# Moving the float32r tiles of an encoder layer to multiples of 512 bytes

## Chip, core and metric

The kernel runs on one core of one Trainium2 chip. The metric is the device time of one execution in microseconds (us). Before the change three runs took 2624.37, 2624.96 and 2625.81 us; the median, 2624.96, is the time to compare with.

## What is computed

One encoder layer on 256 tokens of 2048 channels, in float32. `lnorm` is a layer norm, ALPHA is 2 ** 0.25.

```python
h = lnorm(ALPHA * h + 0.5 * swiglu(h, ffn1_w_in, ffn1_w_out))   # d_ff = 5632
proj = h @ mix_w_in                                             # 2048 x 18944
y_a = hgrn2_both_directions(proj[...]) @ w_a                    # 16 heads of 128
y_b = dilated_attention(proj[...]) @ w_b                        # 3 groups of 4 heads
h = lnorm(ALPHA * h + (g_a * y_a + g_b * y_b) @ mix_w_out)
h = lnorm(ALPHA * h + 0.5 * swiglu(h, ffn2_w_in, ffn2_w_out))
```

All large products are of a [256, K] activation with a weight matrix that is read once from memory, 474 MB in all.

## The kernel before

**Precision.** Every operand of a large product is split into a high and a low part, both of type float32r (`H` is the value rounded to float32r, `L` is what is left), and the product is the sum of three: high by high, high by low, low by high. Activations are kept transposed, channels on partitions: `xH`/`xL` (input of a stage), `hH`/`hL` (hidden layer of a swiglu), `zH`/`zL` (gated sum of the mixer), `oBH`/`oBL` (attention output).

**Order of the work.** `Job` (line 43) is one block of output columns. `run` (line 181) walks through the jobs and cuts the weights of each into chunks of 2048 values per partition, 1 MB. `load` (line 148) fetches a chunk with one DMA into `raw` (three buffers), and splits it, half by half, into `wH` (ScalarE) and `wL` (VectorE, line 165), four buffers of each. `run` loads the chunks of one step ahead. A chunk of a block of 1024 columns feeds 24 matmuls of 512 columns at line 217: two rows of 128 channels, three products, two token tiles of 128, two halves of the block. The activation is the stationary operand (128x128) and the weights are the moving one (128x512):

```python
nc.tensor.matmul(out=job.ps[t, j], lhsT=job.lhs(a, k, t),
                 rhs=b[:, o + j * 512:o + (j + 1) * 512], start=first, stop=last)
```

In the jobs marked `dims` (line 229) it is the other way round: weights stationary, 256 columns of `xH` or `xL` moving. In the attention's projection `lhs` is `parity` (line 762): every second token, so the stationary operand is read with a step of two elements. Each matmul instruction comes with its own load of the stationary operand, also where two in a row use the same one.

The last chunks of three jobs (`room` in `load`, lines 400 and 925) don't have their split weights in `wH`/`wL` but in tiles called `early`, which lie in other pools.

The recurrence and the attention itself work on float32 tiles (lines 653 to 687, 808, 816), and `transpose4` (line 101) transposes with the identity matrix `ident` as the moving operand.

**Where the tiles lie.** Pools are stacked in the order in which they are opened, and a pool's tiles in the order in which their names first appear. The tile `ident` is at byte 16512 of each partition. Behind it come the other constants, `vecs` (512 bytes) among them, then the pools `wraw` (`raw`), `wsp` (`wH`, `wL`), `big` (`acc`, `xH`, `xL`), `small` (statistics and scratch, 1248 bytes), and from byte 127520 on the pools of the stages. So the starting addresses, as remainders of a division by 512 and by 64, are:

| tiles | pool | mod 512 | mod 64 |
|---|---|---|---|
| `raw`, `wH`, `wL`, `acc`, `xH`, `xL` | wraw, wsp, big | 320 | 0 |
| `hH`, `hL`, `silu`, `early`, `zH`, `zL`, `oBH`, `oBL`, `z` | pools of the stages | 32 | 32 |
| `ident` | const | 128 | 0 |
| float32 tiles of the recurrence | hgrn | 288, 320 or 352 | 32, 0 or 32 |

Within a tile all operands of line 217 start at multiples of 512 bytes (128 tokens of 4 bytes, or 512 columns), but for `parity`, whose second token tile starts 4 bytes later than the first.

The change touches the constants and pools at lines 86 to 92 and the line `vecs = const.tile(...)` at 426. `vecs` holds five short vectors that are loaded, transposed once (`lower_bounds`) and not used again, all in the first microseconds of the kernel.

Of the kernel before, what the change touches and what calls it, by code (L numbers as in the profile page):

```python
# [10 lines left out]
F32 = mybir.dt.float32  # L11
# [6 lines left out]
P = 128  # L18
# [24 lines left out]
class Job:  # L43
    """One block of output columns: out[tok, C] = sum over nk tiles of x^T W.

    head/tail: this many of the first/last chunks run one token tile after the other.
    room: gives room for a chunk's split weights outside the pool for them, or None.
    mid: called after the first step; hook: before the last token tile meets the last chunk.
    dims: the block comes out transposed, out[col, tok], two heads to a bank.
    """  # L50

# [18 lines left out]
def kernel(ctx, tc, x, ffn1_in, ffn1_out, ln1_g, ln1_b, mix_in, lb_fwd, lb_bwd,  # L70
# [3 lines left out]
    x, out = x[0], out[0]  # L74
# [3 lines left out]
    const = ctx.enter_context(tc.tile_pool(name="const", bufs=1))  # L78
# [3 lines left out]
    small = ctx.enter_context(tc.tile_pool(name="small", bufs=2))  # L82
# [9 lines left out]
    acc = big.tile([P, NT, D], F32, name="acc")  # L92

    def new_x():
        return (big.tile([P, KD, SEQ], F32R, tag="xH", name="xH"),
                big.tile([P, KD, SEQ], F32R, tag="xL", name="xL"))
# [4 lines left out]
    def transpose4(srcs):  # L101
        ps = tp_tile()
        for i, s in enumerate(srcs):
            nc.tensor.transpose(out=ps[:, i * P:(i + 1) * P], in_=s, identity=ident)  # L104
        return ps

    def split(ps, H, L):
        """H + L = ps exactly, both in float32r."""
        nc.scalar.copy(out=H, in_=ps)  # L109
        nc.vector.tensor_sub(out=L, in0=ps, in1=H.bitcast(F32))  # L110

    def rsqrt(y, v, n):
        """y = v ** -0.5 for [P, n] (v is positive): a guess from the exponent and three Newton steps."""
        z = small.tile([P, n], F32, tag=f"rs{n}", name="rsz")
        nc.vector.tensor_scalar(y.bitcast(I32), v.bitcast(I32), 1, None, op0=OP.logical_shift_right)
        nc.vector.tensor_scalar(y.bitcast(I32), y.bitcast(I32), -1.0, MAGIC, op0=OP.mult, op1=OP.add)
        for i in range(3):
            if n == 1:
                nc.vector.scalar_tensor_tensor(z, y, v, y, op0=OP.mult, op1=OP.mult)
            else:  # L120
                nc.vector.tensor_mul(z, y, y)
                nc.vector.tensor_mul(z, z, v)
            # the factor -2 of each of the first two steps stays in y, and is taken out in the last
            if i < 2:
                nc.vector.scalar_tensor_tensor(y, z, -3.0 * 4.0 ** i, y, op0=OP.add, op1=OP.mult)
            else:
                nc.vector.tensor_scalar(z, z, -768.0, -1.0 / 8192.0, op0=OP.add, op1=OP.mult)
                return nc.vector.tensor_mul(y, y, z)
# [17 lines left out]

# [1 line left out]
    def load(job, r, parts=1):  # L148
# [25 lines left out]
    def fence(ins):  # L174
        """What is traced from here to the end of this step or, if that is sooner, of the next
        goes to the vector engine behind ins."""
        es = ExitStack()
        es.enter_context(tc.issue_after(ins.ins))
        fences.append([es, 2])
# [95 lines left out]
    def to_x(src, xo, t, c):  # L275
        """Columns c * 512... of token tile t, in src [P, 512], to the transposed H and L."""
        ps = transpose4([src[:, i * P:(i + 1) * P] for i in range(4)])
        ts = slice(t * P, (t + 1) * P)
        split(ps.rearrange("p (k s) -> p k s", k=4), xo[0][:, 4 * c:4 * c + 4, ts], xo[1][:, 4 * c:4 * c + 4, ts])

# [1 line left out]
    stats = {}  # L282
# [6 lines left out]
    class LayerNorm:  # L289
# [32 lines left out]
        def tile(self, t):  # L322
            """Token tile t of acc is complete."""
            if t == 1:
                for c, u in self.got.items():
                    self.apply(0, c, u)
            self.begin(t)
            if t == 0:
                if not self.lead:
                    self.apply(0, 0)  # L330
            elif self.dst is not None:
                self.rest([(1, c) for c in range(4)])
            elif self.lead:
                self.rest([(1, 0), (1, 1), (0, 2), (1, 2), (0, 3), (1, 3)])
            else:
                self.rest([(1, 0)] + [(tt, c) for c in range(1, 4) for tt in range(NT)])

        def first(self):
            """The last tile is nearly complete."""
            for c in range(2 if self.dst is None else 4):  # L340
                self.got[c] = self.scale(0, c)
# [10 lines left out]

# [1 line left out]
    def ffn(w_in, w_out, cur, pool, before, tpost, post, hook):  # L354
# [66 lines left out]

# [1 line left out]
    cur["x"] = new_x()  # L423
    pl = {}
    pl["ffn"] = open_pool("ffn1")
    vecs = const.tile([P, P], F32, name="vecs")

# [53 lines left out]

# [1 line left out]
    ln = {}  # L483
# [19 lines left out]

# [1 line left out]
    hs = {}  # L505
# [42 lines left out]
    def hgrn_pair(g, pr, st):  # L548
# [15 lines left out]
        def flat(ap, t, b, f):  # L564
            """[P, h * t, u] or, for one t, [P, h, u] of half f of block b."""
            if t is None:
                return ap.rearrange("p (g b f u) -> p g b f u", b=2, f=2, u=HCHUNK)[:, :, b, f, :]
            return v6(ap)[:, :, t, b, f, :]
# [4 lines left out]
        q = st["q", pr]  # L573
        f = {0: st["f", pr], 1: st["b", pr]}
        d1s, d1e = hs["d1s"], hs["d1e"]
        K1, Q1, KC, QC = t512("k1"), t512("q1"), t512("kc"), t512("qc")
        # direction d: inc is the decay from the chunk's entry up to and with a token, exc the decay
        # from behind a token to the chunk's end; entry and end are those of the direction's time
        KS, QR, inc, K2, Q2 = {}, {}, {}, {}, {}
        for d in range(2):  # L580
            k = t512("k")
# [3 lines left out]
            a = inc[d] = t512(f"i{d}")  # L585
# [17 lines left out]
            yield 1.7  # L603
            # near half: the one that the direction enters first
            nr, fr = (0, 1) if d == 0 else (1, 0)
# [6 lines left out]
        for d in range(2):  # L612
            # keys of block bk meet queries of block bq of the same tile, keys of tile bk queries of tile bq
            nr, fr = (0, 1) if d == 0 else (1, 0)
            bk, bq = nr, fr
            T = inc[d].rearrange("p (c u) -> p c u", u=HCHUNK)[:, :, 31:32] if d == 0 else c32(inc[d])[:, :, 0:1]
# [26 lines left out]

        # scores, keys on partitions
        def tok(ap, h, t):
# [28 lines left out]
        ATo = p.tile([P, 2, 2, P], F32, tag="ato", name="ato")  # L674
# [3 lines left out]
        for h in range(2):  # L678
            hl = 2 * pr + h
            hd = 4 * g + hl  # L680
            v = st["v"]
            for t in range(NT):
                o = po[:, (2 * h + t) * P:(2 * h + t + 1) * P]
                nc.tensor.matmul(out=o, lhsT=ATd[h][:, t, :], rhs=v[:, t, hl * P:(hl + 1) * P],  # L684
                                 start=True, stop=False)
                # ATo[:, h, 0]: keys of tile 0, queries of tile 1; [:, h, 1] the other way
                nc.tensor.matmul(out=o, lhsT=ATo[:, h, 1 - t, :], rhs=v[:, 1 - t, hl * P:(hl + 1) * P],  # L687
                                 start=False, stop=True)
# [70 lines left out]

    # attention: columns of group g are q, k, v of 512; tile 0 has the even tokens and tile 1 the odd ones,  # L760
    # so that the second and third group attend only within a tile
    def parity(x, k, t):
# [75 lines left out]

    # branch gates
    def gate_evac(key, blk):  # L840
# [95 lines left out]
    for blk in range(2):  # L936
        jobs.append(Job(mix_out, 0, KD, blk * 1024, 1024, lambda: (hs["zH"], hs["zL"]), mo_evac(blk),
                        tpost=ln2_tile if blk == 1 else None, post=ln2 if blk == 1 else None, tail=4 * blk,
                        room=ln2_room if blk == 1 else None, hook=lambda: ln[2].first()))

# [1 line left out]
    def ln3_before():  # L942
        ln[3] = LayerNorm(load_gb(pl["ffn"], ln3_g[0], ln3_b[0]), pl["ffn"], None, out, lead=True)

    ffn2 = ffn(ffn2_in, ffn2_out, cur, lambda: pl["ffn"], ln3_before, lambda t: ln[3].tile(t), close_pool,
               lambda: ln[3].first())
# [53 lines left out]
```

## Time and profile before

| | |
|---|---|
| median of three runs | 2624.96 us |
| span of the profiled execution, first to last instruction | 2623.6 us |
| TensorE matmul busy | 2600.1 us, 99%, 12889 instructions |
| TensorE load of the stationary operand busy | 2187.8 us, 83%, 12889 instructions |
| VectorE busy | 1533.4 us, 58% |
| ScalarE busy | 1155.7 us, 44% |
| DMA | 483 MB, 184 GB/s, 54% of the engines' time |
| mean granted TensorE clock | 0.999 |

The page gives no other time for the profiled execution than its span, so what lies around the span is taken as its distance to the median, 1.4 us. The records of two successive matmuls overlap (a matmul of 512 columns has a record of about 390 ns, and the next one begins before it ends). The time that a matmul costs is therefore not its duration but the distance from its start to the next one's start: the length of a stretch in which TensorE never idles, divided by the number of matmuls that start in it.

### The profile page before, as it was taken

The page shows a single profiled execution, that of the slowest core. Times are in us where ns is not written, and L with a number is a line of the kernel's source. Part 1 is how long each engine was busy: PE and PEld are TensorE (multiplying, and loading weights), DVE is VectorE, ACT ScalarE, POOL GpSimd, SP SyncE. Part 2 cuts the span into 40 slices and gives each one's busy share as a digit, 9 for nine tenths or more (in the row PEclk, how much of TensorE's full clock was granted, in tenths as well). Part 3 has the DMA queues.
Part 4 walks back from the last instruction along what each step waited for, and adds up shares of the span by engine and source line. Part 5 has one row for each costly group of instructions (what it writes and reads, how often), then busy time and mean ns, then how long its engine had stood idle before and what let it go on. Part 6 is the DMA issues. An engine that isn't in the chain of part 4 may idle for free.

```text
span 2623.6 us, 31518 instructions
## 1 busy us (share of the span) xinstructions
PE 2600.1 (99%) x12889; PEld 2187.8 (83%) x12889; DVE 1533.4 (58%) x1865; ACT 1155.7 (44%) x1395; POOL 4.8 (0%) x28
## 2 busy tenths in 40 slices
PE   8999999999999999999999999999999999999998
PEld 7888888888889999998888888888788888888886
DVE  5455555454585877878544544556755455555557
ACT  5444343444444455554544544444444444444442
POOL 0000000000000000000000000000000000000000
PEclk9999999999999999999999999999999999999999
DMA  7555555555655544544555445656555555555563
GB/s 243 187 184 192 192 192 179 193 190 192 211 174 177 177 162 145 174 163 161 188 177 183 154 162 193 191 191 213 172 193 191 193 178 192 191 192 181 193 220 129
DMA packets 147281, 483.32 MB, mean 184 GB/s; under 512 B 7664, under 2 KB 7872, under 8 KB 146368
## 3 DMA queue, kind: packets, MB, share of 16 engines
q1 hardware_dynamic: 145680, 473.99, 54.4%
q10 hardware_dynamic: 1456, 7.32, 0.7%
q8 instruction: 101, 1.65, 0.2%
q14 instruction: 44, 0.36, 0.0%
HBM read 479.17 MB, written 2.10 MB: 183 GB/s over the span
## 4 chain that ended last, share of the span: by engine, by line
PE 97%; DVE 2%; DMA 0%; ACT 0%; issue 0%; SPq 0%; DVEq 0%; ACTq 0%
PE ps L217 82%; PE ps L229 10%; PE tp L104 2%; PE tp L653 1%; PE tp L657 1%; DVE wL L165 0%; DVE lnu L307 0%; PE tp L687 0%; DVE lnu L311 0%; DMA acc<-in_x 0%; PE tp L808 0%; PE tp L816 0%; DVE st L287 0%; PE tp L684 0%; PE tp L672 0%; ACT wH L165 0%
## 5 line engine op out<-in xcount | busy, mean ns | idle before, releaser
L165 DVE TENSOR_TENSOR wL<-raw,wH 128x1024 fp32r<-128x1024 f32 x884 | 1078.1, 1222 | 1007.8 <-ACT wH L165 1006.3
L165 ACT CAST wH<-raw 128x1024 fp32r<-128x1024 f32 x884 | 929.0, 1052 | 1291.5 <-PE ps L217 1157.0
L217 PE MATMUL ps<-wH,xH 128*128 128x512 f32 x2336 | 748.1, 391 | 1.7 <-ACT xH L109 1.7
L217 PE MATMUL ps<-wL,xH 128*128 128x512 f32 x2336 | 749.0, 391 | 0.0
L217 PE MATMUL ps<-wH,xL 128*128 128x512 f32 x2336 | 748.6, 391 | 0.3
L217 PEld LDWEIGHTS ps<-wH,xH 128*128 128x128 f32 x2336 | 440.0, 189 | 92.5 <-ACT xH L109 2.8
L217 PEld LDWEIGHTS ps<-wH,xL 128*128 128x128 f32 x2336 | 440.2, 189 | 92.1 <-DVE xL L110 1.8
L217 PEld LDWEIGHTS ps<-wL,xH 128*128 128x128 f32 x2336 | 439.6, 189 | 89.9
L217 PE MATMUL ps<-wL,hH 128*128 128x512 f32 x672 | 216.7, 399 | 0.0
L217 PE MATMUL ps<-wH,hH 128*128 128x512 f32 x672 | 212.0, 396 | 0.0
L217 PE MATMUL ps<-wH,hL 128*128 128x512 f32 x672 | 210.9, 395 | 0.0
L217 PEld LDWEIGHTS ps<-wH,hL 128*128 128x128 f32 x672 | 126.0, 188 | 29.8
L217 PEld LDWEIGHTS ps<-wH,hH 128*128 128x128 f32 x672 | 125.2, 188 | 29.7
L217 PEld LDWEIGHTS ps<-wL,hH 128*128 128x128 f32 x672 | 125.3, 188 | 29.0
L229 PE MATMUL ps<-xH,wH 128*128 128x256 f32 x768 | 125.8, 285 | 0.0
L229 PE MATMUL ps<-xL,wH 128*128 128x256 f32 x768 | 124.8, 284 | 0.0
L229 PE MATMUL ps<-xH,wL 128*128 128x256 f32 x768 | 124.8, 284 | 0.0
L229 PEld LDWEIGHTS ps<-xH,wH 128*128 128x128 f32 x768 | 106.5, 192 | 0.3
L229 PEld LDWEIGHTS ps<-xH,wL 128*128 128x128 f32 x768 | 106.3, 192 | 0.0
L229 PEld LDWEIGHTS ps<-xL,wH 128*128 128x128 f32 x768 | 106.3, 192 | 0.0
L385 DVE SCALAR_TENSOR_TENSOR acc<-ps,acc 128x512 f32<-128x512 f32 x96 | 60.3, 680 | 1.3 <-PE ps L217 1.3
L217 PE MATMUL ps<-wL,zH 128*128 128x512 f32 x112 | 35.4, 397 | 0.0
(181 smaller groups left out, 1244.7 us busy)
## 6 DMA issues: line engine op xcount, KB each, us to landing
raw<-in_ffn_w_in SPq DMA_DIRECT2D x175, 1024.0 KB, 5.0
raw<-in_mix_w_in SPq DMA_DIRECT2D x148, 1024.0 KB, 5.1
raw<-in_ffn_w_out SPq DMA_DIRECT2D x88, 1024.0 KB, 5.3
raw<-in_w_branch_a SPq DMA_DIRECT2D x16, 1024.0 KB, 5.3
raw<-in_mix_w_out SPq DMA_DIRECT2D x16, 1024.0 KB, 5.4
raw<-in_w_branch_b SPq DMA_DIRECT2D x4, 1024.0 KB, 5.3
gbt<-in_ln_g ACTq DMA_DIRECT2D x3, 1024.0 KB, 7.2
gbt<-in_ln_b ACTq DMA_DIRECT2D x3, 1024.0 KB, 10.0
```

What stands on the lines that cost most here:

```text
L104: nc.tensor.transpose(out=ps[:, i * P:(i + 1) * P], in_=s, identity=ident)
L165: both = nc.scalar.copy(out=H, in_=s), nc.vector.tensor_sub(out=L, in0=s, in1=H.bitcast(F32))
L217: nc.tensor.matmul(out=job.ps[t, j], lhsT=job.lhs(a, k, t), rhs=b[:, o + j * 512:o + (j + 1) * 512], start=first, stop=last)
L229: nc.tensor.matmul(out=job.ps[h // 2][:, (h % 2) * SEQ:(h % 2 + 1) * SEQ], lhsT=b[:, o + h * P:o + (h + 1) * P], rhs=a[:, k, :], start=fir ...
L385: nc.vector.scalar_tensor_tensor(a, ps, 0.5, a, op0=OP.mult, op1=OP.add)
L653: nc.tensor.matmul(out=pa[:, (d * NT + t) * P:(d * NT + t + 1) * P], lhsT=tok(KS[d], h, t), rhs=tok(QR[d], h, t), start=True, stop=True)
L657: nc.tensor.matmul(out=pc[:, (i * NT + t) * P:(i * NT + t + 1) * P], lhsT=tok(a, h, t), rhs=tok(b, h, t), start=True, stop=True)
```

## The change

Two tiles are added that nothing writes or reads: `fill` of 48 float32 values (192 bytes) among the constants, and `fill` of 72 values (288 bytes) at the front of `small`. `vecs` moves from the constants to the front of the pool `ffn1`. Everything behind the constants thus moves down by 320 bytes and everything behind `small` by 32. Addresses after: `raw`, `wH`, `wL`, `acc`, `xH`, `xL` and all of `hH`, `hL`, `silu`, `early`, `zH`, `zL`, `oBH`, `oBL`, `z` start at a multiple of 512. `ident` stays at 128. The float32 tiles of the recurrence go from 288, 320, 352 to 256, 288, 320. The strided second token tile of `parity` starts at 4. No instruction is added, removed or given another operand; the rest of the diff takes out comments.

```diff
     acc = big.tile([P, NT, D], F32, name="acc")
 
+    const.tile([P, 48], F32, name="fill")
+    small.tile([P, 72], F32, name="fill", bufs=1)
+
     def new_x():
...
     pl["ffn"] = open_pool("ffn1")
-    vecs = const.tile([P, P], F32, name="vecs")
+    vecs = pl["ffn"].tile([P, P], F32, name="vecs")
```

## Rows read from the trace of the kernel before

**Rows 1.** The page's busy times by engine.
```profile
span 2623.6 us, 31518 instructions
...
PE 2600.1 (99%) x12889; PEld 2187.8 (83%) x12889; DVE 1533.4 (58%) x1865; ACT 1155.7 (44%) x1395; POOL 4.8 (0%) x28
```

**Rows 2.** The page's chain of work that ended last, shares of the span by engine.
```profile
PE 97%; DVE 2%; DMA 0%; ACT 0%; issue 0%; SPq 0%; DVEq 0%; ACTq 0%
```

**Rows 3.** Who waited for whom on TensorE: us in total, times, longest.
```profile
PE tp L104 <- DMA acc<-in_x: 8.6, 2, 4.3
PE ps L217 <- ACT xH L109: 1.7, 4, 0.4
PE tp L104 <- ACT ast L774: 0.2, 1, 0.2
```

**Rows 4.** Busy time of each engine in three stretches in which TensorE does nothing but matmuls of line 217: the first with `xH`/`xL` as stationary operand, the second with `hH`/`hL`, the third with `oBH`/`oBL`; `wH`/`wL` moves in all. After the length come busy us and, in brackets, the instructions of PE, PEld, DVE, ACT and POOL, then the granted clock, the DMA engines' busy share and GB/s. The edges lie just ahead of a load, so the number behind PEld is that of the loads and thus of the matmuls that start in the stretch.
```profile
304.80:391.85 87.05, 87.05 (x385) 72.07 (x384) 43.71 (x41) 35.81 (x36) 0.00 (x0) 1.00 0.58 191
2392.10:2433.16 41.06, 41.06 (x177) 32.99 (x176) 21.50 (x21) 15.25 (x15) 0.00 (x0) 1.00 0.59 190
1668.14:1690.30 22.16, 22.16 (x96) 17.81 (x95) 16.91 (x17) 12.47 (x14) 0.00 (x0) 1.00 0.60 190
```

**Rows 5.** Timeline of TensorE's matmuls around the first chunk of `early` (moving) with `hH`/`hL` (stationary): start, us, instruction, count. The chunk begins at 733.65 and ends at 739.12.
```profile
733.65 1.09 PE L217 MATMUL ps<-early,hH 128*128 128x512 f32 x4
734.58 0.62 PE L217 MATMUL ps<-early,hL 128*128 128x512 f32 x2
735.04 1.07 PE L217 MATMUL ps<-early,hH 128*128 128x512 f32 x4
735.94 0.61 PE L217 MATMUL ps<-early,hL 128*128 128x512 f32 x2
736.40 0.62 PE L217 MATMUL ps<-early,hH 128*128 128x512 f32 x2
736.85 0.39 PE L217 MATMUL ps<-early,hL 128*128 128x512 f32 x1
737.08 0.62 PE L217 MATMUL ps<-early,hH 128*128 128x512 f32 x2
737.53 0.39 PE L217 MATMUL ps<-early,hL 128*128 128x512 f32 x1
737.76 0.62 PE L217 MATMUL ps<-early,hH 128*128 128x512 f32 x2
738.21 0.39 PE L217 MATMUL ps<-early,hL 128*128 128x512 f32 x1
738.44 0.62 PE L217 MATMUL ps<-early,hH 128*128 128x512 f32 x2
738.89 0.39 PE L217 MATMUL ps<-early,hL 128*128 128x512 f32 x1
739.12 0.63 PE L217 MATMUL ps<-wH,hH 128*128 128x512 f32 x2
```

**Rows 6.** Pieces of the chain that ended last, in order of time: start, us, what, matmuls. The first is a stretch of the recurrence's projection (256 columns moving), the second one of the attention's, with `parity` as stationary operand.
```profile
778.52 69.11 PE ps L229 x576
1359.56 43.87 PE ps L217 x188
```

**Rows 7.** Groups of instructions, matmuls by operands: count behind the x, then busy us and the mean ns of one record.
```profile
L217 PE MATMUL ps<-wL,xH 128*128 128x512 f32 x2336 | 749.0, 391 | 0.0
L217 PE MATMUL ps<-wL,hH 128*128 128x512 f32 x672 | 216.7, 399 | 0.0
L217 PE MATMUL ps<-wL,zH 128*128 128x512 f32 x112 | 35.4, 397 | 0.0
L217 PE MATMUL ps<-wL,oBH 128*128 128x512 f32 x32 | 10.1, 395 | 0.0
L229 PE MATMUL ps<-xL,wH 128*128 128x256 f32 x768 | 124.8, 284 | 0.0
```

**Rows 8.** The same view, the splitting of weights and activations on VectorE and ScalarE, into tiles at either place: count, busy us, mean ns, idle time before and who ended it.
```profile
L165 DVE TENSOR_TENSOR wL<-raw,wH 128x1024 fp32r<-128x1024 f32 x884 | 1078.1, 1222 | 1007.8 <-ACT wH L165 1006.3 <-DMA vecs<-in_hgrn_norm_g 0.6
L165 ACT CAST wH<-raw 128x1024 fp32r<-128x1024 f32 x884 | 929.0, 1052 | 1291.5 <-PE ps L217 1157.0 <-PE ps L229 108.3 <-issue 17.5
L165 DVE TENSOR_TENSOR early<-raw,early 128x1024 fp32r<-128x1024 f32 x12 | 14.1, 1218 | 3.3 <-ACT early L165 3.3
L165 ACT CAST early<-raw 128x1024 fp32r<-128x1024 f32 x12 | 12.0, 1049 | 6.2 <-DMA raw<-in_ffn_w_out 4.2 <-DMA raw<-in_mix_w_out 2.0
```

**Rows 9.** DMA issues: count, KB of one, median us from issue to landing.
```profile
raw<-in_ffn_w_out SPq DMA_DIRECT2D x88, 1024.0 KB, 5.3
```

## The prediction

> **What bounds the kernel now.** I read the busy times first: TensorE's matmuls cover 99% of the span [rows 1], and the chain that ended last is TensorE for 97% [rows 2]. TensorE hardly waits for anybody: 10.5 us in all, nearly all of it for the first input [rows 3]. So only two things can move the time much: fewer matmuls, of which the change has none, or less time from one matmul's start to the next. The question is whether that distance depends on where the operands lie, and the trace of before can answer it, because it already holds tiles at two kinds of places: 320 past a multiple of 512 bytes (a multiple of 64) and 32 past one.
>
> The second view is the stretches in which TensorE never idles [rows 4]. With `xH`, both operands at 320, 384 matmuls take 87.05 us: 226.7 ns each. With `hH`, stationary at 32 and moving still at 320, 176 take 41.06 us: 233.3 ns. With `oBH`, the same pair of places, 95 take 22.16 us: 233.3 ns. [...] So a matmul whose stationary operand lies at 32 costs 6.6 ns more.
>
> The third view tells which property does it. In the chunk with `early` as the moving operand [rows 5] both operands lie at 32, and from 735.04 to 739.12 us 18 matmuls take 4.08 us: 226.7 ns, as with both at 320. The same `hH` is dear with weights at 320 and cheap with weights at 32. So the price is not that of a tile at an odd place, but of two operands at **different** places; the load of one matmul's stationary operand runs while another's moving operand is being read, and the two seem to get in each other's way unless they are in step.
>
> [...]
>
> **The change, part by part.**
>
> *The places.* Afterwards all float32r tiles start at multiples of 512. Both operands of line 217 are then in step wherever the stationary one isn't strided, and I take the price of pairs in step, 226.7 ns, which two different places show [rows 4, 5].
>
> *How many gain.* Matmuls with a stationary `hH`/`hL`, `zH`/`zL` or `oBH`/`oBL` and `wH`/`wL` moving: three products each of 672, 112 and 32 [rows 7] make 2448. Some 40 of them follow a transpose or a chunk of `early`, and I leave them out: 2410. Gain 2410 x 6.6 = **15.9 us**, all of it on the path, since TensorE is the path. From below, counting the whole `early` chunk with its uneven start, 733.65 to 739.12, 24 matmuls take 5.47 us, 227.9 ns; the gain would be 2410 x 5.4 = 13.0 us.
>
> *Those already in step.* 2336 x 3 less the strided ones with `xH`, and 768 x 3 of 256 columns [rows 7], go from 320/320 to 0/0. No row shows a start at a multiple of 512. Two places that agree in nothing but being in step give one price, so I take no change; the bounds are the two rivals below.
>
> *The strided loads.* The attention's projection has 9 x 512 columns by 16 rows of channels by three products by two token tiles, 864 matmuls. They take 43.87 / 188 = 233.4 ns [rows 6], although their loads start at 320 or 324 with the moving operand at 320: a step of two goes out of step anyway. I take no change. Bounds: all come down to 226.7, 864 x 6.7 = 5.8 us gained, or as much lost.
>
> *Other engines.* Splitting a half chunk takes 1222 and 1052 ns into tiles at 320, 1218 and 1049 ns into `early` at 32 [rows 8]; VectorE and ScalarE don't care. I cost their moved tiles at nothing; both wait for TensorE for a large part of the span (ScalarE 1157 us [rows 8]), which is the cover.
>
> *The weight stream.* A faster TensorE asks for chunks sooner in the `hH` stretches: 24 x 226.7 = 5.44 us for a chunk instead of 5.60. A chunk of that matrix lands 5.3 us after its issue [rows 9] with three buffers in flight, and the `xH` stretch already runs at 5.44 us per chunk with a DMA share of 0.58 [rows 4]. So the gain isn't taken back by a late chunk. If this cover were gone, every chunk would take what it takes now and the gain would be zero.
>
> *The float32 tiles and the transposes.* The recurrence's tiles change places, `ident` does not. Together with the moved `vecs`, whose loads and transpose keep their instructions and queues, I cost them at nothing; a microsecond either way is possible and lies inside the bounds above.
>
> **Sum.** Profiled span 2623.6 - 15.9 = 2607.7 us; with the 1.4 us by which the median stands above that span, **2609.1 us**. Bounds: 13.0 - 5.8 = 7.2 us gained at least, 15.9 + 5.8 = 21.7 at most, so 2603.3 to 2617.8. What a measurement of this kernel can tell from no change is about 0.2%, 5.2 us.
>
> **The rivals.**
>
> *A. The multiple of 512 itself counts, and helps.* From 256 to 512 columns a matmul goes from 69.11 / 576 = 120.0 ns [rows 6] to 226.7, 106.7 for 256 columns. So 512 columns alone are 213.3 ns, and every float32r matmul carries 13.3 ns more, whatever its length. Both places of the trace make a 512-byte load run over a multiple of 512; after the change none does, and these 13.3 ns could be such a crossing. There are 9,600 matmuls of 512 and 2,304 of 256 columns: all of it gone would be another 11,904 x 13.3 = 158 us, 2451 us; half of it, 2530 us. For it: nothing in the trace excludes it. Against it: 320 and 32 cross at different points of the load and cost the same to a tenth of a nanosecond. I give it 0.10.
>
> [...]
>
> *B. Nothing happens.* Either the unused tiles get no room, so that everything stays at 320 and 32, or the price in the `hH` stretches comes from what else runs there and `early` is cheap by accident. Against it: three stretches at 233.3 to 233.4, two at 226.7, and VectorE busy in the cheap and the dear ones. Time 2625.0. I give it 0.08. [...]
>
> *C. Starting at a multiple of 512 makes moving reads and loads collide.* Place: the same matmuls that are now in step, 11,904 - 2,410 - 864 = 8,630. It decides from 15.9 us / 8,630 = 1.8 ns per matmul on; at one more step of 6.6 ns it costs 57 us, and with the gain lost too the time is 2682. For it: that addresses matter at all. Against it: the operands in step move on by 512 bytes from one row or tile to the next, and no stretch shows a dear member in such a series. I give it 0.05.
>
> **How the numbers follow.** The forecast has 0.77. Its own range, 2603 to 2618, leaves out more than 2 in 10, so the range reaches on to the nearest other case, no change: 2603 to 2625 holds 0.77 and most of B. Faster by over 0.2%: the forecast with A, 0.87. Within 0.2%: B, 0.08. Slower: C, 0.05.
>
> **What would show it.** Right: in the changed trace the stretches with `hH`, `zH` and `oBH` show 226.7 ns like those with `xH`; the `xH` stretches and the 256-column ones stay at 226.7 and 120.0; the strided ones stay near 233; waits of TensorE and the clock stay as they are; the span falls by about 16 us. Wrong: `xH` stretches below 226 (A), `hH` stretches still at 233 (B), `xH` stretches above 228 (C), or a new wait of line 217 for `wH` or `wL`, which would mean that the stream and not the address set the pace.

## The result, and the profile after

The changed kernel takes 2610.36 us (median of 4 runs, 2610.26 to 2611.34), the kernel before beside it 2625.39 us; the ratio is 0.9944, with a 95% interval of 0.9929 to 0.9958. That is 15.0 us less; 15.9 were forecast. The profiled span went from 2623.6 to 2608.2 us.

The page's busy times, the kernel after (before: [rows 1]):

```profile
span 2608.2 us, 31519 instructions
...
PE 2585.7 (99%) x12889; PEld 2188.4 (84%) x12889; DVE 1533.2 (59%) x1865; ACT 1156.7 (44%) x1395; POOL 4.7 (0%) x28
```

Matmuls got 14.4 us shorter in sum, with the same number of them; the sums of the other engines moved by 1.0 us at most. The one instruction more in the page's count is a semaphore instruction of GpSimd. The lines of the code moved by three, so line 217 is now 220 and 229 is 232. Here are the stretches that answer to [rows 4], with `xH`, `hH` and `oBH` as stationary operand, and a fourth with `zH`; the columns are the same, and again the number behind PEld is that of the matmuls that start in the stretch:

```profile
302.17:388.76 86.59, 86.59 (x383) 71.70 (x382) 43.34 (x41) 35.80 (x36) 0.00 (x0) 1.00 0.58 192
2379.96:2419.67 39.71, 39.71 (x176) 32.85 (x175) 21.18 (x21) 15.34 (x15) 0.00 (x0) 1.00 0.58 194
1661.14:1682.45 21.31, 21.31 (x95) 17.64 (x94) 16.52 (x17) 12.52 (x14) 0.00 (x0) 1.00 0.58 189
1779.57:1843.99 64.42, 64.42 (x285) 53.30 (x284) 37.89 (x37) 27.72 (x28) 0.00 (x0) 1.00 0.71 246
```

The distance from one matmul's start to the next is 86.59 / 382 = 226.7 ns with `xH`, as before, and now 39.71 / 175 = 226.9 with `hH`, 21.31 / 94 = 226.7 with `oBH`, 64.42 / 284 = 226.8 with `zH`. The dear stretches came down to the cheap ones; the cheap ones stayed. The 256-column stretch and the strided one stayed as well, as the pieces of the chain that answer to [rows 6] show:

```profile
771.62 69.11 PE ps L232 x576
...
1352.61 43.86 PE ps L220 x188
```

The records of single matmuls tell the same by a few ns, 399 to 394 for `wL` with `hH` and 397 to 392 with `zH` [rows 7]; their mean hides most of it, since successive records overlap. The groups after, by operands (count, busy us, mean ns):

```profile
L220 PE MATMUL ps<-wL,hH 128*128 128x512 f32 x672 | 213.1, 394 | 0.0
...
L220 PE MATMUL ps<-wL,zH 128*128 128x512 f32 x112 | 34.8, 392 | 0.0
```

No wait took the place of the gain, and the granted clock is 1.00 in all four stretches, as before. TensorE's waits after, which answer to [rows 3], are 9.7 us in all; the one for `wL` is of a transpose of the first input, not of line 220:

```profile
PE tp L107 <- DMA acc<-in_x: 4.0, 1, 4.0
PE tp L107 <- DVE wL L168: 3.0, 1, 3.0
PE ps L220 <- ACT xH L112: 1.7, 4, 0.4
PE tp L107 <- DVE lnu L314: 0.5, 2, 0.3
PE ps L220 <- DVE xL L113: 0.3, 2, 0.2
PE tp L107 <- ACT ast L777: 0.2, 1, 0.2
```

### The profile page after: what moved, and what is told of

The parts are those of the page before. It is cut to its first block, busy times and chain, and to the rows that moved or that the text cites. A ratio compares the mean times of both kernels' runs of the same rounds, so it can differ in the third digit from the quotient of the medians.

```text
span 2608.2 us, 31519 instructions
## 1 busy us (share of the span) xinstructions
PE 2585.7 (99%) x12889; PEld 2188.4 (84%) x12889; DVE 1533.2 (59%) x1865; ACT 1156.7 (44%) x1395; POOL 4.7 (0%) x28
## 4 chain that ended last, share of the span: by engine, by line
PE 96%; DVE 3%; ACT 0%; DMA 0%; issue 0%; DVEq 0%; ACTq 0%
PE ps L220 82%; PE ps L232 11%; PE tp L107 2%; PE tp L656 1%; PE tp L660 1%; DVE wL L168 1%; DVE lnu L310 0%; PE tp L690 0%; DVE st L290 0%; DVE lnu L314 0%; PE tp L811 0%; PE tp L819 0%; PE tp L687 0%; DVE acc L388 0%; ACT wH L168 0%; DMA raw<-in_ffn_w_out 0%
## 5 line engine op out<-in xcount | busy, mean ns | idle before, releaser
L220 PE MATMUL ps<-wH,zL 128*128 128x512 f32 x112 | 34.8, 390 | 0.0
```

What stands on the lines that cost most here:

```text
L220: nc.tensor.matmul(out=job.ps[t, j], lhsT=job.lhs(a, k, t), rhs=b[:, o + j * 512:o + (j + 1) * 512], start=first, stop=last)
```

## The experiments

What the trace of before couldn't say was which property of the new places pays: the multiple of 512, or that both operands are at the same place; what "the same" means (modulo 64, 256 or 512); and which two operands have to agree. The step of a matmul is here the distance from the moving operand's place to the stationary one's; in step means a distance that costs nothing. Where no range or interval stands beside a time, it is of a single run.

**One part of the change at a time.** First the spare tile in `small` alone, which brings every float32r tile to 320, where the weights already were:

```diff
     acc = big.tile([P, NT, D], F32, name="acc")
+    small.tile([P, 72], F32, name="fill", bufs=1)
```

> The kernel before with the 288-byte spare tile in small alone: all float32r tiles start at 320 past a multiple of 512, none at a multiple. Theory (only the step between the moving operand and the stationary operand loaded meanwhile counts): hH, zH and oBH stretches at 226.7 ns, time 2610 us, the whole gain. Rival (the multiple of 512 itself counts): less than the whole gain, hH stretches between 227 and 233 ns, time 2611 to 2625 us.

Then the other part alone, `vecs` moved and `fill` in `const`, without the tile in `small`:

```diff
     const.tile([P, 48], F32, name="fill")
-    small.tile([P, 72], F32, name="fill", bufs=1)
```

> The other part alone: raw, wH, wL, acc, xH and xL at multiples of 512, hH, zH, oBH and early at 224 past one, which is 32 past a multiple of 64. Theory (step): nothing gained, hH stretches at 233.3 ns, early chunks at 226.7, time 2625 us. Rival (it is enough that the moving operand starts at a multiple of 512): hH stretches below 230 ns, time below 2618 us.

The first took 2610.74 us (2610.34 to 2611.69, ratio 0.9945, 0.9932 to 0.9958), the second 2625.20 us (ratio 1.0, 0.999 to 1.0009). So the whole gain comes from one spare tile of 288 bytes, without a single float32r tile at a multiple of 512, and moving the weights to multiples of 512 by itself does nothing. The `xH` and `hH` stretches, of the first kernel:

```profile
2287.64:2374.23 86.59, 86.59 (x383) 71.72 (x382) 43.35 (x41) 35.81 (x36) 0.00 (x0) 1.00 0.58 191
2379.96:2419.67 39.71, 39.71 (x176) 32.86 (x175) 21.18 (x21) 15.34 (x15) 0.00 (x0) 1.00 0.60 195
```

and of the second:

```profile
2299.18:2385.77 86.59, 86.59 (x383) 71.70 (x382) 43.26 (x41) 35.80 (x36) 0.00 (x0) 1.00 0.58 191
2391.51:2432.34 40.82, 40.82 (x176) 32.80 (x175) 21.24 (x21) 15.24 (x15) 0.00 (x0) 1.00 0.57 191
```

226.7 and 226.9 ns in the first, 226.7 and 40.82 / 175 = 233.3 in the second, where `xH` and `wH` start at multiples of 512 and only `hH` doesn't.

**The cheap chunk made dear.** The forecast read the rule from chunks with `early` as the moving operand [rows 5]. If they were cheap for another reason, moving `early` must not change them:

```diff
-            return [pool().tile([P, RAW], F32R, tag=("early", "silu")[r - 2], name="early", bufs=2) for _ in range(2)]
+            return [pool().tile([P, RAW + 16], F32R, tag=("early", "silu")[r - 2], name="early",
+                                bufs=2)[:, 8:8 + RAW] for _ in range(2)]
```

> The kernel before, with the moving early tiles of the two swiglus 32 bytes further on, thus at a multiple of 64, while hH and hL stay 32 past one. Theory (step): the early chunks with hH go from 226.7 to about 233 ns; the others stay, total up by 96 x 6.6 ns = 0.6 us. Rival (these chunks are cheap because of what else runs, or because early lies in another pool): they stay at 226.7.

Measured: 2627.27 us in one run, and in the trace a chunk of the moved `early` with `hH` and one of the unmoved `early` with `zH`:

```profile
733.98:739.10 5.12, 5.12 (x23) 4.13 (x22) 4.48 (x8) 0.00 (x0) 0.00 (x0) 1.00 0.86 314
1854.24:1859.25 5.01, 5.01 (x23) 4.13 (x22) 0.88 (x2) 0.00 (x0) 0.00 (x0) 1.00 0.86 309
```

5.12 / 22 = 232.7 ns against 5.01 / 22 = 227.7. The step makes the price here too. The edit moved more than `early`, though: the second pair of `early` tiles shares its buffers with `silu`, and these got wider with it. So the four `early` tiles came to 64, 128, 192 and 256, and `hH` and `hL`, which lie behind `silu`, went from 32 to 160. That made the other `hH` stretches dearer as well:

```profile
396.84:437.83 40.99, 40.99 (x176) 32.96 (x175) 21.25 (x21) 15.28 (x15) 0.00 (x0) 1.00 0.57 189
```

40.99 / 175 = 234.2 ns instead of 233.3, about 0.9 ns on each of some 2000 matmuls, 1.8 us. So the total, 1.7 us above the kernel before beside it (2625.54) where 0.6 were expected, says nothing on the `early` chunks.

**The other way round.** Everything as in the changed kernel, but `acc`, `xH` and `xL` 32 bytes further on:

```diff
+    big.tile([P, 8], F32, name="fill")
     acc = big.tile([P, NT, D], F32, name="acc")
...
-    small.tile([P, 72], F32, name="fill", bufs=1)
+    small.tile([P, 64], F32, name="fill", bufs=1)
```

> The changed kernel with acc, xH and xL 32 bytes past a multiple of 512, weights and all else at multiples. Theory (step): xH stretches from 226.7 to about 233.3 ns, 6,089 x 6.6 = 40 us; the 256-column ones from 120.0 to 126.6 if a load costs the same there, 2,274 x 6.6 = 15 us; the strided ones unknown. Total about 2665 us, slower than both kernels. Rival (the price belongs to the stages and not to the places): xH stretches stay at 226.7, time 2610 us.

Measured: 2641.30 us, slower than the kernel before (ratio 1.0063, 1.0041 to 1.0086), but 24 us less than expected. Its `xH`, `hH` and strided stretches:

```profile
309.35:398.48 89.13, 89.13 (x383) 71.77 (x382) 43.42 (x41) 35.74 (x36) 0.00 (x0) 1.00 0.56 187
404.18:443.87 39.70, 39.70 (x176) 32.85 (x175) 21.17 (x21) 15.35 (x15) 0.00 (x0) 1.00 0.60 195
1364.10:1407.26 43.17, 43.17 (x187) 36.37 (x186) 19.30 (x19) 17.65 (x19) 0.00 (x0) 1.00 0.57 186
```

and its 256-column piece of the chain:

```profile
786.36 67.20 PE ps L233 x576
```

`xH` went from 226.7 to 89.13 / 382 = 233.3 ns and `hH` stayed at 39.70 / 175 = 226.9: the price follows the places. But with 256 columns a step of 32 bytes is cheaper: 67.20 / 576 = 116.7 ns against 120.0. The sum goes by that, with the counts of the expectation: 6,089 x 6.6 = 40 us more, 2,274 x 3.3 = 7.5 less, 864 x (233.3 - 43.17 / 186 = 1.2) = 1.0 less, together 31.5; measured 2641.3 - 2610.4 = 30.9. That the 6.6 ns hold for every shape was a false extension.

**Which modulus.** Each of the twelve blocks of the two swiglus got another place for `hH` and `hL` (`PHASE` is the list of the offsets in bytes):

```diff
+                o = PHASE[len(phases) % 12] // 4
+                phases.append(o)
+                for n, nm in (("H", "hH"), ("L", "hL")):
+                    a = pool().tile([P, 8 * SEQ + 64], F32R, tag=nm, name=nm, bufs=2)
+                    st[n] = a[:, o:o + 8 * SEQ].rearrange("p (k s) -> p k s", k=8)
```

> The changed kernel, hH and hL of the twelve blocks of the two swiglus start 0, 4, 8, 16, 32, 48, 0, 64, 128, 96, 60 and 12 bytes past a multiple of 256, weights at multiples of 512. Theory, with a unit of 64 bytes: 226.7 ns at 0, 64 and 128, about 233 at 32, 96, 16, 48, 4, 8, 12 and 60, total about 2621 us. Rival one, a unit of 32 bytes or less would make 32 and 96 cheap (excluded by the kernel before, if 288 is what counts there). Rival two, a unit of 512: 64 and 128 are dear too, about 233.

Total 2619.91 us. The second buffers lay 256 bytes past a multiple of 512, so the places were 260 (offset 4), 8, 320 (offset 64), 128, and, in the kernel's last block, 268 (offset 12; its last 24 matmuls with `wH` and `wL`); the stretches in that order:

```profile
262.18:302.85 40.67, 40.67 (x176) 32.82 (x175) 21.25 (x21) 15.24 (x15) 0.00 (x0) 1.00 0.59 190
395.63:436.00 40.37, 40.37 (x176) 32.88 (x175) 21.23 (x21) 15.30 (x15) 0.00 (x0) 1.00 0.58 192
2119.89:2160.72 40.83, 40.83 (x176) 32.91 (x175) 21.25 (x21) 15.29 (x15) 0.00 (x0) 1.00 0.57 190
2253.52:2294.35 40.83, 40.83 (x176) 32.85 (x175) 21.25 (x21) 15.23 (x15) 0.00 (x0) 1.00 0.58 189
2594.63:2600.07 5.44, 5.44 (x25) 4.50 (x24) 5.02 (x17) 0.00 (x0) 0.00 (x0) 1.00 0.00 2
```

232.4, 230.7, 233.3, 233.3 and 5.44 / 24 = 226.7 ns. A unit of 64 is out: places 320 and 128 are multiples of 64 and dear. The 268 at 226.7 was a surprise. The second series had buffers of a multiple of 512 (128 spare values each):

> The changed kernel, hH and hL of the twelve blocks 480, 64, 128, 192, 256, 24, 320, 384, 448, 12, 268 and 264 bytes past a multiple of 512, weights at multiples of 512. By now a unit of 64 has failed (in e3_phases 64 and 128 were dear). Theory, a unit of 512: all twelve dear, 230 to 235 ns, unless some odd step falls between two collisions, as 268 did in e3_phases (226.7). Rival, a unit of 256: 256 is as cheap as 0, 226.7, and 12 as cheap as 268. Total about 2621 to 2623 us.

Total 2618.55 us, below the 2621 to 2623 expected, since not all twelve were dear. Stretches with places 64, 128, 192, 256, 384, 448 and 12:

```profile
262.21:303.05 40.84, 40.84 (x176) 32.90 (x175) 21.24 (x21) 15.29 (x15) 0.00 (x0) 1.00 0.57 189
395.86:436.52 40.67, 40.67 (x176) 32.97 (x175) 21.26 (x21) 15.27 (x15) 0.00 (x0) 1.00 0.58 190
529.30:569.36 40.06, 40.06 (x176) 32.87 (x175) 21.21 (x21) 15.30 (x15) 0.00 (x0) 1.00 0.59 193
662.17:701.87 39.69, 39.69 (x176) 32.84 (x175) 21.19 (x21) 15.32 (x15) 0.00 (x0) 1.00 0.73 245
2118.70:2159.52 40.83, 40.83 (x176) 32.85 (x175) 21.27 (x21) 15.24 (x15) 0.00 (x0) 1.00 0.59 190
2252.33:2292.39 40.06, 40.06 (x176) 32.86 (x175) 21.22 (x21) 15.30 (x15) 0.00 (x0) 1.00 0.58 193
2385.18:2426.02 40.84, 40.84 (x176) 33.02 (x175) 21.27 (x21) 15.23 (x15) 0.00 (x0) 1.00 0.58 190
```

Divided by 175: 233.4, 232.4, 228.9, 226.8, 233.3, 228.9 and 233.4 ns. The block at 256 is as cheap as one at 0. Places that differ by 256 pair up: 192 and 448 to the hundredth, 64 and the 320 above, 384 and the 128 above (in this run 128 had 232.4); 128 and 64 are dear, so no smaller power of two will do. That speaks for 256. The test over the whole kernel puts all stationary operands of line 220 at 256 and the weights at 0:

```diff
+    big.tile([P, 64], F32, name="fill")
     acc = big.tile([P, NT, D], F32, name="acc")
```

> The changed kernel with a spare tile of 256 bytes ahead of acc: raw, wH and wL at multiples of 512, acc, xH, xL and all tiles of the stages 256 past one, so that the operands of every matmul are 256 apart. Theory (operands keep step if they agree modulo 256): time as the changed kernel's, 2610 us, all stretches at 226.7 and 120.0 ns. Rival (512): all of the 8,600 contiguous matmuls dear, 2667 us.

2610.82 us (2610.51 to 2611.21), ratio 0.9945 (0.9928 to 0.9961): as fast as the changed kernel. Its `xH` and `hH` stretches:

```profile
302.83:389.42 86.59, 86.59 (x383) 71.70 (x382) 43.35 (x41) 35.81 (x36) 0.00 (x0) 1.00 0.57 192
2380.56:2420.28 39.71, 39.71 (x176) 32.84 (x175) 21.17 (x21) 15.34 (x15) 0.00 (x0) 1.00 0.59 194
```

226.7 and 226.9 ns. In these runs operands kept step where their places agree modulo 256; the rival of 512, 2667 us, is out.

**Which two operands.** In one kernel `wL` and `hL` moved by 32 bytes. The padding of 64 bytes per buffer did more than that: it put the four `wL` buffers at 32, 96, 160 and 224, everything behind them at 256, and the two `hL` buffers at 288 and 352, so that `wL` and `hL` agree modulo 256 in one `wL` buffer of four only.

```diff
-                L = wsp.tile([P, HALF], F32R, tag="wL", name="wL")
+                L = wsp.tile([P, HALF + 16], F32R, tag="wL", name="wL")[:, 8:8 + HALF]
```

> The changed kernel with wL and hL 32 bytes further on, all else in step. Two ways to count pairs. Theory (a matmul's distance to the next depends on its own moving operand and the stationary operand of the next matmul, which is loaded meanwhile): in hH stretches 2 of 6 distances are dear, 226.7 + 6.6/3 = 228.9 ns on average; xH stretches also 228.9. Rival (a matmul's own two operands count): in hH stretches 4 of 6 are dear, 231.1 ns; xH stretches 228.9. Total by the theory 2610 + 13.4 (xH) + 4.4 (hH) + 5.1 (256 columns) + 0.7 (zH, oBH) = 2634 us, by the rival 2638.

Measured: 2645.85 us, more than either count gives. In the `hH` stretches pairs that were to be in step weren't, so those can't judge between the counts. In the `xH` stretches one product of three, `wL` with `xH`, is out of step by either count:

```profile
308.05:396.44 88.39, 88.39 (x383) 71.72 (x382) 43.35 (x41) 35.66 (x36) 0.00 (x0) 1.00 0.56 188
```

88.39 / 382 = 231.4 ns, 4.7 more than in step where a third of 6.6 is 2.2. A cleaner kernel moved `hL` alone, with buffers of a multiple of 512:

```diff
+                a = pool().tile([P, 8 * SEQ + 128], F32R, tag="hL", name="hL", bufs=2)
+                st["L"] = a[:, 8:8 + 8 * SEQ].rearrange("p (k s) -> p k s", k=8)
```

> The changed kernel with hL alone 32 bytes past a multiple of 512. Which two operands make a pair? Theory (the matmul's moving operand and the next matmul's stationary one): of a round of six, the second matmul of wL with hH and the first of wH with hL are dear, the second of wH with hL is cheap. Rival (a matmul's own two operands): both of wH with hL are dear, both of wL with hH cheap. Either way 2 of 6, total about 2615 us.

2619.89 us instead of 2615, and this is the rhythm in an `hH` stretch, start, us, what, count:

```profile
400.41 0.62 PE L220 MATMUL ps<-wH,hH 128*128 128x512 f32 x2
400.87 0.63 PE L220 MATMUL ps<-wL,hH 128*128 128x512 f32 x2
401.34 0.62 PE L220 MATMUL ps<-wH,hL 128*128 128x512 f32 x2
401.80 0.63 PE L220 MATMUL ps<-wH,hH 128*128 128x512 f32 x2
```

A round of six takes 401.80 - 400.41 = 1.39 us, 231.7 ns each; both theories gave 1.37. And it isn't one pair that is dear: 0.46, 0.47 and 0.46 us for `wH`/`hH`, `wL`/`hH` and `wH`/`hL`, where two matmuls in step take 0.453. These rows are rounded to 0.01 us; the starts of single matmuls in the trace, averaged over the 29 rounds from 395.9 to 436.3 us, put the six distances of a round at 230.5 to 235.0 ns, the longest from the second `wL`/`hH` to the first `wH`/`hL`. Here one operand out of step made also its neighbours dear that are in step. Both theories of pairs failed.

**One step, one price?** The step of 12 had been cheap once and dear twice. So all twelve blocks got it (the same edit with one value):

> The changed kernel with hH and hL of all twelve blocks 12 bytes past a multiple of 512. A step of 12 was cheap in one stretch of e3_phases and dear in two of e7_phases512. Theory one (a step has one price): all hH stretches near 233.2 ns, total about 2623 us. Theory two (loads can fall into more than one rhythm, and how a stretch begins decides): some stretches near 226.7, others near 233, total between 2611 and 2623 us.

2619.68 us in one run. Three stretches of it, of the same shape and the same step; the first and the third read operands at the very same bytes, in the same order:

```profile
263.33:303.58 40.24, 40.24 (x176) 32.79 (x175) 21.22 (x21) 15.25 (x15) 0.00 (x0) 1.00 0.58 192
396.36:436.60 40.24, 40.24 (x176) 32.79 (x175) 21.23 (x21) 15.28 (x15) 0.00 (x0) 1.00 0.58 193
529.40:570.24 40.84, 40.84 (x176) 33.02 (x175) 21.27 (x21) 15.23 (x15) 0.00 (x0) 1.00 0.58 190
```

229.9, 229.9 and 233.4 ns, with the other engines and the DMAs alike. The starts of single matmuls show the rhythm: in the first two the distances alternate between 236 and 224 ns, in the third they repeat 229, 235, 240 and 229. So one step can run in more than one rhythm, each kept for a whole stretch; the second theory holds in that, though the lower price was 230 here and not 226.7. The operands' places don't select the rhythm: in the first and the third stretch they are the same, and a matmul costs 229.9 ns in the one and 233.4 in the other. What selects it wasn't found.

**A kernel that goes further.** The strided loads of the attention's projection still cost 233.3 ns. They exist because queries, keys and values are projected in the order of parity. Queries, keys and the first group's values can be projected in natural order, if ScalarE reorders the transposed queries and keys on its way out of PSUM:

```diff
     def parity(c0):
         def lhs(x, k, t, j):
             idx = c0 // 512 + j
             return x[:, k, t::NT] if idx in (5, 8) else rows(x, k, t)
         return lhs
...
+                    nc.scalar.copy(out=T.rearrange("p h (r s) -> p h r s", r=NT)[:, :, :, t * 64:(t + 1) * 64],
+                                   in_=ps2.rearrange("p (h s r) -> p h r s", h=AHEADS, r=NT))
```

The constant tables of positions and of the first group's mask follow the natural order.

> The changed kernel, with the attention's queries and keys and the first group's values projected in the natural order of tokens, so that 672 of the 864 strided loads become contiguous; the order by parity is made when ScalarE writes the transposed queries and keys (a strided read of PSUM). Theory (a load that keeps step saves 6.6 ns): 672 x 6.6 = 4.4 us less than the changed kernel, 2606 us. Rival (the slower copies on ScalarE hold up the transposes, or strided loads were dear for another reason): 2610 us or more.

> The changed kernel once more, beside e8_natural_qk on the same chip: 2610 us.

2607.13 us (2606.76 to 2607.40, five runs) against 2610.67 (2610.20 to 2611.12, five runs) for the changed kernel beside it; the two don't overlap. Their ratios to the kernel before are 0.9931 (0.9918 to 0.9943) and 0.9944 (0.9930 to 0.9957). The gain is 3.5 us of the 4.4 expected. Two stretches of the projection, now contiguous:

```profile
1263.89:1302.47 38.58, 38.58 (x171) 31.91 (x170) 17.47 (x17) 17.18 (x21) 0.00 (x0) 1.00 0.61 199
1395.77:1437.95 42.19, 42.19 (x187) 34.91 (x186) 19.22 (x17) 17.51 (x19) 0.00 (x0) 1.00 0.56 183
```

38.58 / 170 = 226.9 and 42.19 / 186 = 226.8 ns. From the first start of the projection to the last it is 207.4 us, against 211.4 in the trace of the changed kernel, so 3.9 of the 4.4 are in the projection. One block mixes strided loads and contiguous ones: there the distances alternate between 224 and 236 ns, 230.1 on average, so contiguous loads among strided ones didn't reach 226.7. What took the rest isn't known. This version is faster than both kernels.

## Why the prediction was right, point by point

- **The bound.** TensorE was the path, so what its matmuls gained showed in the time. Shown: 14.4 us less busy time, 15.4 us less span, no new wait of line 220 for `wH` or `wL`.
- **The price of a step, 6.6 ns, and the 2410 matmuls.** Shown in size, a little high: the stretches with `hH`, `zH` and `oBH` fell from 233.3 to 226.7 to 226.9. Over all 2404 matmuls of these groups whose next one starts within 260 ns, the mean distance fell from 233.22 to 227.15 ns, 14.6 us where the sum had 15.9: the stretch from 394.5 to 434.2 us, in step, ran at 227.2 in its first half and reached 226.7 only in its second. Of the 15.4 us in the span 0.8 are shorter waits, and in the trace of `after_again` the waits were 10.7 us again. No luck was needed: the 6.6 ns were measured at the very step that the change takes away.
- **That being in step is what counts, and not the place.** Shown: 320/320 (e1) gave the whole gain, 2610.74 us, 0 against 224 (e2) gave none, 2625.20, and moving the cheap tile made it dear (e4, 232.7 ns). Modulo what the places have to agree the prediction didn't say; it had no need to, since the change puts all at one place.
- **Those already in step, nothing.** Shown, 226.7 and 120.0 before and after. Rival A's 13.3 ns of every matmul, an estimate from those two, have nothing to do with these places; where they come from stays open.
- **Strided loads, nothing.** Shown, 233.4 before and 233.3 after. Its bound, 5.8 us if all 864 came down, wasn't tried; contiguous loads in place of 672 saved 3.5 us (e8).
- **The weight stream and the other engines.** Shown: ScalarE and VectorE have the same busy time to 1.0 us (1155.7 and 1156.7, 1533.4 and 1533.2), and no chunk was waited for in the `hH` stretches.
- **Rivals B and C.** B is out by the result: matmuls of one kind differ with the distance of their two operands' places, 233.3 against 226.7 ns in e2, 233.3 against 226.9 in e6. C is out, since starts at a multiple of 512 cost what those at 320 do, 226.7 ns with `xH` in both.
- **What was argued beyond the rows.** That one matmul's load and another's moving read get in each other's way was an argument, and the simplest form of it is wrong: no count of pairs explains e9 (1.39 us a round where both gave 1.37), and the same operands at the same bytes have two prices in e10 (229.9 and 233.4). That loads run beside matmuls is shown, 2188.4 and 2585.7 us busy in a span of 2608.2; the address effect is shown; its mechanism isn't.

## What to carry to other kernels

When TensorE is the path, divide gapless stretches by their matmuls, one stretch for each pair of operand tiles; if equal shapes differ by some per cent, compare the places of the two operands modulo 256: here 256 bytes apart cost 226.7 ns (e11), 32 apart 233.3 (e6). In this kernel a spare tile that brought stationary and moving float32r tiles to equal places, with 512 columns moving, was worth 0.6%, and which place it was did not matter, 2610.74 us at 320 (e1) and 2610.36 at 0. Measure it for each shape: at 256 columns 32 bytes out of step saved 3.3 ns a matmul (e6). And work out what a padding moves: in e4 and e5 wider buffers also moved the tiles behind them.

## What the runs showed of the hardware that was not expected

- Out-of-step distances settled at a few values, 233.3 to 233.4 most often (steps of 12, 32, 64, 128, 224, 320 and 384), 234.2 (96 modulo 256, in e4), 232.4, 230.7 and 228.9 (192 and 448).
- With 256 columns moving, 32 bytes out of step was cheaper than in step, 116.7 ns (e6) against 120.0 (the changed kernel).
- A rhythm lasted for a stretch (e10): with the same operands at the same bytes two stretches of one kernel ran at 229.9 and 233.4 ns, the one with distances of 236 and 224 ns in turn, the other with 229, 235, 240 and 229.
- Where all loads of a stretch read the stationary operand with a step of two elements, a matmul cost 233.3 ns at an equal place (the changed kernel) and 232.1 with 32 bytes between (e6).
